# Output projection of a backbone layer: seven block products in another order, with other sums in PSUM

## The chip, the cores and the metric

The kernel runs on one core of a Trainium2 chip. The metric is device time in microseconds of one execution, and lower is better. The engines are named as in the profile: PE does the matmuls (PEld its weight loads), DVE the elementwise work on vectors, ACT the casts, copies, squares and roots, POOL (GpSimd) elementwise work in memory, and SP issues most transfers. PE writes its results to PSUM, which has eight banks; a bank holds 128 x 512 float32 values.

## The reference, cut to what matters

One layer: modulation, an input projection, a gated convolution and a neighbourhood attention side by side, a gated merge of the two branches, one output projection, a root-mean-square norm and a residual addition. Only the last steps are touched:

```python
merged = jax.nn.sigmoid(g_a) * y_a + jax.nn.sigmoid(g_b) * y_b
y = merged @ w_o                                  # (512, 1024) @ (1024, 1024)
x = x + gt[:, None, :] * _rmsnorm(y, post_g[i])
```

All of it is float32. The kernel writes a float32 operand as a high and a low part of a reduced type (F32R), and a product of two such operands as three matmuls: high by high, high by low, low by high.

## The kernel before

`layer` works in stages: modulation and norm, the input projection, attention, and then the stretch that matters here: the **merge** (the loop over `j` at L715, eight steps) and the **output projection** behind it (from L759).

*Merge.* Step `j` computes 128 of the 1024 merged features, transposed (features on partitions, the 512 tokens along the free axis). Two units of 24 matmuls each (L115 to L117, in `step_T`) multiply a chunk of 256 weight columns by the split operands `us` and `as`; L719 multiplies each result by its gate, and L726 adds the two to `m2[j]`. For `j` below 6 the gates of step `j + 2` are computed too (`merge_gates`, two more units, with the operands `h`). A chunk of weights is loaded by SP into `raw` (L84), cast on ACT (L70) and subtracted on DVE (L71), which gives its high and low part in a buffer `w`; there are two such buffers. `split` at L67 is the helper for all of these pairs, so L70 and L71 stand for every cast and every rest in the profile, told apart by the tile.

*Output projection.* The merged matrix is taken as 2 x 2 blocks (A11 and A12: the first 256 tokens by the first and last 512 features; A21 and A22: the last 256 tokens), and so is the weight `wo` (B11, B12, B21, B22, each 512 x 512, held as two tiles of 128 x 1024). Instead of eight block products there are seven (a scheme of the Strassen kind), on sums of blocks:

- row sums, made on DVE from the `m2` tiles: X1 = A22 - A21, S2 = -(X1) - A11, S3 = A11 - A21, S4 = -S2 - A12, up to sign;
- weight sums T1 to T4, made on DVE in place from the B tiles (`add_to`, L767);
- `moving` (L759) splits a weight block into a `w` buffer (two casts and two rests of 128 x 1024); `operand` and `split` do it for a row sum.

`both` issues one block product as two products of 12 matmuls (L773), one for each 128 tokens. The seven pairs follow one another: A11 B11 (bank pair `fa`), S3 T3 (`fd`), A12 B21 (`fb`), X1 T1 (added to `fd`), S2 T2 (added to `fa`), A22 T4 (added to `fa`), S4 B22 (added to `fd`). In between, ACT copies a running PSUM sum aside (`snap`, L801: P1s, P7s, U2s), and DVE adds such a copy to another bank to get a block of the output `ys` (L850, L864, L870, L875, L882). POOL subtracts P7s from U2s (L867). The last product is done in two halves of 256 columns (L881), both in the bank `fd[1]`, with L882 reading a half behind each.

*Norm and store.* `squares` (L803) has ACT square a block and sum it along the row (L804), and multiplies the block by `gpost` on POOL or DVE (L806). `partial` (L808) and `close` (L815) turn the sums into the reciprocal root of each row (a square root on ACT, L817, a reciprocal on DVE, L818), and L820 scales the row, adds the residual `xr` and leads to the store (L824).

What sets the order: each engine runs its instructions in one fixed order, in which the compiler's planner put them: it goes through the program in the order written and may take a later instruction first where an earlier one is not ready by its own estimate. So an instruction in the profile can stand far from its place in the text. A tile with a tag that another tile used before waits until the earlier one is no longer read. Reads and writes of the same PSUM bank are kept apart too, whichever columns they touch.

Of the kernel before, what the change touches and what calls it, by code (L numbers as in the profile page):

```python
# [27 lines left out]
def layer(ctx: ExitStack, tc, xp, ctxt, ctxT, cc, wmod, small, wfirst, win, wout, wo, rel, tab, out):  # L28
# [684 lines left out]
    h0, h1 = slice(0, 256), slice(256, S)

    for j in range(KT):  # L715
        w = chunk()
        g = G[j]
        for i in range(2):
            nc.vector.scalar_tensor_tensor(  # L719
                out=g[i], in0=g[i], scalar=1.0, in1=unit(w, i, ua[i]), op0=ALU.add, op1=ALU.mult  # L720
            )
# [4 lines left out]
        nc.vector.tensor_add(m2[j], g[0], g[1])  # L726
        if j < 4:
            split(A11[j // 2][:, 0, j % 2], A11[j // 2][:, 1, j % 2], m2[j][:, h0])
        if j == 1 or j == 3:
            q = j // 2  # L730
            x = cv.tile([P, S], F32, name="tb").rearrange("p (k c) -> p k c", k=2)
            nc.vector.tensor_sub(x, raws[q][:, :, h0], raws[q][:, :, h1])
            split(S3[q][:, 0], S3[q][:, 1], x)
        if j < 6:
            for _ in merge_gates(j + 2):
                pass
        if j == 4:

            nc.vector.tensor_scalar(out=gains[:, 0:4], in0=gains[:, 0:4], scalar1=0.5, scalar2=None, op0=ALU.mult)
            nc.vector.tensor_scalar(out=gains[:, 4:8], in0=gains[:, 4:8], scalar1=-0.5, scalar2=None, op0=ALU.mult)  # L740
            gpost = bp.tile([P, D], F32, name="gpost")
            for i in range(2):
                gb = cv.tile([P, S], F32, name="ta")
                ps = pj()
                for k in range(4):
                    n = 4 * i + k
                    nc.vector.tensor_copy(gb[:, k * P:(k + 1) * P], gains[:, n:n + 1].broadcast_to([P, P]))
                    nc.tensor.transpose(ps[:, k * P:(k + 1) * P], gb[:, k * P:(k + 1) * P], ident)
                nc.scalar.copy(gpost[:, i * S:(i + 1) * S], ps)
        if j == 5:  # L750

            B = {}
            for n, (r, c) in enumerate(((0, 0), (0, 1), (1, 1), (1, 0))):
                B[r, c] = [hp.tile([P, 2, S], F32, name=f"B{r}{c}{q}", tag=f"h{2 * n + q}") for q in range(2)]
                for q in range(2):
                    k = 4 * r + 2 * q
                    nc.sync.dma_start(B[r, c][q], wo[c, :, k:k + 2])

    def moving(src):  # L759
        t = wp.tile([P, 2, 4, S], F32R, name="w", bufs=2)  # L760
        for q in range(2):
            split(t[:, 0, 2 * q:2 * q + 2], t[:, 1, 2 * q:2 * q + 2], src[q])
        return t

    def add_to(dst, src):
        for q in range(2):
            nc.vector.tensor_add(dst[q], dst[q], src[q])  # L767

    def product(ps, a, w, start, t, cols=slice(0, S)):
        ts = slice(t * P, (t + 1) * P)  # L770
        for k in range(4):
            for x, y, o in ((0, 0, 0), (0, 1, 1), (1, 0, 2)):
                nc.tensor.matmul(  # L773
                    ps[:, cols], lhsT=a(x, k, ts), rhs=w[:, y, k, cols], start=start and k + o == 0,
                    stop=k == 3 and o == 2, skip_group_check=True,
                )

# [11 lines left out]
    fa, fd, fb = ([pj() for _ in range(2)] for _ in range(3))

    wB11 = moving(B[0, 0])
    add_to(B[0, 0], B[0, 1])
    add_to(B[0, 1], B[1, 1])
    wT3 = moving(B[0, 1])
    split(A2[3][:, 0], A2[3][:, 1], m2[7])
    for t in (2, 3, 0, 1):
        for i in range(2):
            nc.sync.dma_start(xr[t][i], xp[t * P:(t + 1) * P, i * S:(i + 1) * S])
# [4 lines left out]
    def squares(t, cols, n, k=1):  # L803
        nc.scalar.activation(sq[:, :cols.stop - cols.start], ys[t][:, cols], AF.Square, accum_out=sums[:, t, n:n + 1])  # L804
# [1 line left out]
        e.tensor_mul(ys[t][:, cols], ys[t][:, cols], gpost[:, cols])  # L806

    def partial(t, n, scalar):  # L808
        d = sums[:, t, 3:4]
        if scalar is None:  # L810
            nc.vector.tensor_scalar(out=d, in0=sums[:, t, n:n + 1], scalar1=0.25 / D, scalar2=EPS, op0=ALU.mult, op1=ALU.add)
# [18 lines left out]
    both(fa, stationary(A11), wB11, True, snap(lambda t: P1s[:, t], fa))  # L830
    wB21 = moving(B[1, 0])
    x2 = [cv.tile([P, S], F32, name="tb").rearrange("p (k c) -> p k c", k=2) for _ in range(2)]
    X1 = operand("X1", bp, ("us4", "us5"))
    S2 = operand("S2", bp, ("us6", "us7"))
    S4 = operand("S4", bp, ("as0", "as1"))
    for q in range(2):
        nc.vector.tensor_sub(x2[q], raws[2 + q][:, :, h1], raws[q][:, :, h1])
        split(X1[q][:, 0], X1[q][:, 1], x2[q])
    both(fd, stationary(S3), wT3, True, snap(lambda t: P7s[:, t], fd))
    wT1 = moving(B[0, 0])  # L840
    for q in range(2):
        nc.vector.scalar_tensor_tensor(
            out=x2[q], in0=x2[q], scalar=-1.0, in1=raws[q][:, :, h0], op0=ALU.mult, op1=ALU.subtract
        )
        split(S2[q][:, 0], S2[q][:, 1], x2[q])
    both(fb, a12, wB21, True)
    add_to(B[0, 0], B[1, 1])
    wT2 = moving(B[0, 0])
    for t in range(2):
        nc.vector.tensor_add(ys[t][:, c0], P1s[:, t], fb[t])  # L850
        squares(t, c0, 0)
        partial(t, 0, None)
    both(fd, stationary(X1), wT1, False)
    add_to(B[0, 0], B[1, 0])
    wT4 = moving(B[0, 0])
    for q in range(2):
        nc.vector.scalar_tensor_tensor(
            out=x2[q], in0=x2[q], scalar=-1.0, in1=raws[2 + q][:, :, h0], op0=ALU.mult, op1=ALU.subtract
        )
        split(S4[q][:, 0], S4[q][:, 1], x2[q])  # L860
    both(fa, stationary(S2), wT2, False, snap(lambda t: U2s[t], fa))
    wB22 = moving(B[1, 1])
    for t in range(2):
        nc.vector.tensor_add(ys[2 + t][:, c1], U2s[t], fd[t])  # L864
# [2 lines left out]
        nc.gpsimd.tensor_sub(U2s[t], U2s[t], P7s[:, t])  # L867
# [5 lines left out]
    s4 = stationary(S4)
    product(fd[0], s4, wB22, False, 0)
    nc.vector.tensor_add(ys[0][:, c1], U2s[0], fd[0])  # L875
    squares(0, c1, 1, 0)
    close(0, 1, ((0, 512), (512, 1024)))
    for i in range(2):
        cols = slice(256 * i, 256 * (i + 1))
        full = slice(S + 256 * i, S + 256 * (i + 1))  # L880
        product(fd[1], s4, wB22, False, 1, cols)  # L881
        nc.vector.tensor_add(ys[1][:, full], U2s[1][:, cols], fd[1][:, cols])  # L882
        squares(1, full, 1 + i, 0)
# [86 lines left out]
```

## Time and profile before

| | us |
|---|---|
| median of 3 runs | 732.17 (731.79 to 732.32) |
| the profiled execution | 731.5 |
| its span, first to last instruction | 729.7 |
| last pair of products of the merge ends, first pair of the projection starts | 677.7 |
| last matmul ends | 723.4 |

The times in the profile's lines are counted from the start of the span. A line of a timeline has the start, the duration of the group (for x2 or more from the first start to the last end), the engine, the line of the kernel, the operation, what it writes and reads, and in brackets how long the engine was idle before it and what released it. Neighbouring operations of one engine overlap a little, so that the distance of their starts is shorter than the duration shown.

### The profile page before, as it was taken

The numbers are of one execution on the slowest core, as the hardware profiler recorded it, in microseconds if no ns is written. First come the engines' busy times: TensorE is split into PE (matmuls) and PEld (weight loads), VectorE is DVE, ScalarE is ACT, GpSimd is POOL, SyncE is SP. The second block draws the span as 40 slices with busy tenths as digits, with TensorE's granted clock in tenths as the row PEclk, the third lists the DMA queues.
The fourth block names the chain that finished last, engine by engine and source line by source line (L and its number), as shares of the span: only waits on it lengthen the run. The fifth ranks groups of instructions, "written<-read, shape, count | busy, mean of one in ns | idle before, by whom it ended". The sixth has DMA issues, their size and how long they took to land.

```text
span 729.7 us, 9349 instructions
## 1 busy us (share of the span) xinstructions
PE 713.5 (98%) x3476; PEld 599.1 (82%) x3476; DVE 544.7 (75%) x1089; ACT 343.5 (47%) x631; POOL 11.6 (2%) x12
## 2 busy tenths in 40 slices
PE   8999999999999999999999999999999999999993
PEld 5888888888888888888888888888888888888882
DVE  7979989996997968779879689674934323326996
ACT  7574523563474654545536446443822222313553
POOL 0000000000000000000000000000000000000041
PEclk9999999999999999999999999999999999999997
DMA  9985982322221222131312212321133233265003
GB/s 351 406 301 180 310 295 91 106 64 92 73 65 67 72 75 71 58 101 44 130 58 74 72 58 73 101 88 58 58 115 114 76 100 116 88 202 201 29 1 116
DMA packets 26544, 86.63 MB, mean 119 GB/s; under 512 B 3073, under 2 KB 3329, under 8 KB 26498
## 3 DMA queue, kind: packets, MB, share of 16 engines
q1 hardware_dynamic: 26354, 85.90, 34.5%
q8 instruction: 27, 0.44, 0.3%
q14 instruction: 19, 0.16, 0.1%
q10 hardware_dynamic: 144, 0.13, 0.1%
HBM read 83.93 MB, written 2.10 MB: 118 GB/s over the span
## 4 chain that ended last, share of the span: by engine, by line
PE 91%; DVE 5%; ACT 1%; issue 1%; DMA 1%; SPq 0%; DVEq 0%; ACTq 0%
PE ps L117 20%; PE ps L115 20%; PE ps L116 20%; PE ps L128 6%; PE ps L600 4%; PE ps L584 4%; PE ps L133 3%; PE ps L552 3%; PE ps L773 2%; PE ps L141 2%; PE ps L307 2%; PE ps L311 2%; PE ps L308 2%; DVE w L71 2%; PE ps L561 1%; PE ps L146 1%
## 5 line engine op out<-in xcount | busy, mean ns | idle before, releaser
L115 PE MATMUL ps<-h,w 128*128 128x512 f32 x528 | 207.5, 393 | 0.0
L117 PE MATMUL ps<-h,w 128*128 128x512 f32 x528 | 206.0, 390 | 0.0
L116 PE MATMUL ps<-h,w 128*128 128x512 f32 x528 | 205.7, 390 | 0.0
L71 DVE TENSOR_TENSOR w<-raw,w 128x1024 fp32r<-128x1024 f32 x90 | 108.2, 1216 | 55.8 <-ACT w L70 55.6
L70 ACT CAST w<-raw 128x1024 fp32r<-128x1024 f32 x90 | 92.3, 1051 | 85.8 <-PE ps L117 64.4
L117 PEld LDWEIGHTS ps<-h,w 128*128 128x128 f32 x528 | 99.1, 188 | 20.9
L116 PEld LDWEIGHTS ps<-h,w 128*128 128x128 f32 x528 | 99.2, 188 | 20.3
L115 PEld LDWEIGHTS ps<-h,w 128*128 128x128 f32 x528 | 99.2, 188 | 20.0
L575 ACT ACTIVATE pt<-ps,m 128x512 f32<-128x512 f32 x64 | 44.3, 694 | 59.6 <-DVE m L572 59.6
L568 DVE CUSTOM_DVE_ANT_1 ps<-ps,bt 128x512 f32<-128x512 f32 x56 | 38.6, 700 | 15.1 <-PE ps L552 12.0
L71 DVE TENSOR_TENSOR TL<-ps,TH 128x512 fp32r<-128x512 f32 x64 | 42.7, 680 | 5.2 <-ACT TH L70 5.2
L719 DVE SCALAR_TENSOR_TENSOR g<-g,ps 128x512 f32<-128x512 f32 x16 | 11.0, 686 | 40.9 <-PE ps L117 40.9
L70 ACT CAST TH<-ps 128x512 fp32r<-128x512 f32 x64 | 35.1, 588 | 6.6 <-PE ps L584 6.4
L633 ACT ACTIVATE g<-ps 128x512 f32<-128x512 f32 x16 | 9.6, 598 | 57.8 <-PE ps L117 57.8
L584 PE MATMUL ps<-ident,pt 128*128 128x128 f32 x256 | 33.3, 272 | 0.0
L128 PE MATMUL ps<-w,h 128*128 128x512 f32 x128 | 32.7, 394 | 0.0
L577 DVE TENSOR_SCALAR pt<-pt,z 128x512 f32<-128x512 f32 x64 | 30.8, 482 | 1.0
L584 PEld LDWEIGHTS ps<-ident,pt 128*128 128x128 f32 x256 | 29.4, 140 | 2.3
L600 PE MATMUL ps<-TH,V 128*128 128x256 f32 (+1 forms) x96 | 28.5, 319 | 0.0
L600 PE MATMUL ps<-TL,V 128*128 128x256 f32 (+1 forms) x96 | 27.7, 318 | 0.0
L517 ACT ACTIVATE qd<-ta 64x512 fp32r<-64x512 f32 x32 | 20.2, 630 | 13.8 <-PE ps L561 7.1
L128 PEld LDWEIGHTS ps<-w,h 128*128 128x128 f32 x128 | 23.1, 189 | 4.3
(181 smaller groups left out, 1194.1 us busy)
## 6 DMA issues: line engine op xcount, KB each, us to landing
raw<-in_win SPq DMA_DIRECT2D x74, 512.0 KB, 4.2
wm<-in_wmod SPq DMA_DIRECT2D x34, 512.0 KB, 6.7
raw<-in_wout SPq DMA_DIRECT2D x16, 512.0 KB, 4.7
bt<-in_rel SPq DMA_DIRECT2D x16, 256.0 KB, 2.6
B<-in_wo SPq DMA_DIRECT2D x8, 512.0 KB, 7.1
fraw<-in_wfirst SPq DMA_DIRECT2D x8, 384.0 KB, 8.7
x<-in_xp SPq DMA_DIRECT2D x4, 512.0 KB, 4.9
xr<-in_xp SPq DMA_DIRECT2D x8, 256.0 KB, 3.0
```

The source lines that it names most:

```text
L70: nc.scalar.copy(H, src)
L71: nc.vector.tensor_sub(L, src, H.bitcast(F32))
L115: nc.tensor.matmul(ps, lhsT=H[:, k, cs], rhs=mH[k], start=k == 0, stop=False)
L116: nc.tensor.matmul(ps, lhsT=H[:, k, cs], rhs=mL[k], start=False, stop=False)
L117: nc.tensor.matmul(ps, lhsT=L[:, k, cs], rhs=mH[k], start=False, stop=k == KT - 1)
L128: nc.tensor.matmul(ps, lhsT=mH[k][:, ts], rhs=both[:, k].rearrange("p a c -> p (a c)"), start=k == 0, stop=False, skip_group_check=True,)
L133: nc.tensor.matmul(ps[:, :256], lhsT=mL[k][:, ts], rhs=H[:, k], start=False, stop=k == KT - 1, skip_group_check=True)
L568: nc.vector.tensor_tensor_reduce(out=s3, in0=s3, in1=bt[:, e::4 - e][:, 0:2], scale=1.0, scalar=-3.0e38, op0=ALU.add, op1=ALU.max, accum_o ...
L575: nc.scalar.activation(pt, s, AF.Exp, bias=m, scale=1.0, accum_out=z)
L577: nc.vector.tensor_scalar(out=pt, in0=pt, scalar1=z, scalar2=None, op0=ALU.mult)
L584: nc.tensor.transpose(tp[:, c], pt[:, c * P:(c + 1) * P], ident)
L600: nc.tensor.matmul(o3[:, dst], lhsT=V[p][:, kt, h], rhs=src(t), start=n == 0 and t is TH, stop=n == len(work) - 1 and t is TL,)
```

## The change

- The seven products come in the order A11 B11 (`fa`), A12 B21 (`fb`), S2 T2 (added to `fa`), X1 T1 (`fe`), S3 T3 (added to `fa`), S4 B22 (added to `fe`), A22 T4 (added to `fa`). The copies taken are P1s, U2s and U3s, all from `fa`. P7s and the two subtractions on POOL are gone.
- Three blocks of the output are an addition of a copy and a bank, as before. The fourth (tokens 256 to 511, first 512 columns) lies complete in `fa` at the end; the square and the product with `gpost` read it from PSUM, without an addition. The exception is the first half of its second 128 tokens, which is computed in a bank of its own (`ff`) and added to U3s.
- The weight sums T1 to T4 are made inside the merge loop at `j == 6`, and have tiles for T2 and T3; B11 and B12 are loaded at `j == 3` into new buffers, B22 and B21 at `j == 5`. T1 overwrites B11 after its split, T4 overwrites B12.
- The row sums X1 and S2 are made in place in the `m2` tiles (`sums1`): for the first half of the features at `j == 5`, for the second after the first product.
- All products with `gpost` are on DVE.
- The size of a DMA scratch area is set to 1024. The residual is loaded in another order.

The diff, cut to its core:

```diff
+    def total(dst, x, y):
+        for q in range(2):
+            nc.vector.tensor_add(dst[q], x[q], y[q])
+    B11, B12 = block("B11", bp, ("B0", "B1")), block("B12", bp, ("B2", "B3"))
+    def sums1(q):
+        nc.vector.tensor_sub(raws[q][:, :, h1], raws[2 + q][:, :, h1], raws[q][:, :, h1])
+        nc.vector.scalar_tensor_tensor(
+            out=raws[q][:, :, h0], in0=raws[q][:, :, h1], scalar=-1.0, in1=raws[q][:, :, h0],
+            op0=ALU.mult, op1=ALU.subtract,
+        )
...
+        if j == 3:
+            load_block(B11, 0, 0)
+            load_block(B12, 0, 1)
...
         if j == 5:
+            sums1(0)
+            B22, B21, T2, T3 = (block(n, hp, (f"h{2 * i}", f"h{2 * i + 1}")) for i, n in enumerate(("B22", "B21", "T2", "T3")))
+            load_block(B22, 1, 1)
+            load_block(B21, 1, 0)
+        if j == 6:
+            wB11 = moving(B11)
+            total(B11, B11, B12)
+            T1 = B11
+            total(T2, T1, B22)
+            total(T3, B12, B22)
+            T4 = B12
+            total(T4, T2, B21)
...
-        e = nc.gpsimd if k else nc.vector
-        e.tensor_mul(ys[t][:, cols], ys[t][:, cols], gpost[:, cols])
+        nc.vector.tensor_mul(y, src, gpost[:, cols])
...
+    both(fa, stationary(A11), wB11, True, snap(P1s, fa))
+    sums1(1)
+    for q in range(2):
+        split(S2[q][:, 0], S2[q][:, 1], raws[q][:, :, h0])
+    wT2 = moving(T2)
+    both(fb, a12, wB21, True)
+    for q in range(2):
+        split(X1[q][:, 0], X1[q][:, 1], raws[q][:, :, h1])
+    wT1 = moving(T1)
+    both(fa, stationary(S2), wT2, False, snap(U2s, fa))
+    wT3 = moving(T3)
...
+    both(fe, stationary(X1), wT1, True)
...
+    def block22(t):
+        snap(U3s, fa)(t)
+        nc.vector.tensor_add(ys[2 + t][:, c1], U3s[:, t], fe[t])
+    both(fa, stationary(S3), wT3, False, block22)
+    wT4 = moving(T4)
...
+    def block12(t):
+        nc.vector.tensor_add(ys[t][:, c1], U2s[:, t], fe[t])
+    both(fe, stationary(S4), wB22, False, block12)
+    for t in range(2):
+        squares(t, c1, 1)
+        close(t, 1, ((0, 512), (512, 1024)))
+    product(fa[0], a22, wT4, False, 0)
+    squares(2, c0, 1, fa[0])
+    close(2, 1, ((0, 512), (512, 1024)))
     for i in range(2):
         cols = slice(256 * i, 256 * (i + 1))
         if i == 0:
+            ff = pj()[:, :256]
+            product(None, a22, wT4, True, 1, cols, ff)
+            nc.vector.tensor_add(ys[3][:, cols], U3s[:, 1, cols], ff)
+            squares(3, cols, 1)
+            partial(3, 1, False)
+        else:
+            product(fa[1], a22, wT4, False, 1, cols)
+            squares(3, cols, 2, fa[1][:, cols])
+    close(3, 2, ((0, 512), (512, 768), (768, 1024)))
...
-    nc = bacc.Bacc("TRN2", target_bir_lowering=False, num_devices=1)
+    nc = bacc.Bacc("TRN2", target_bir_lowering=False, num_devices=1, dynamic_dma_scratch_size=1024)
```

More of the change, by code (lines that the diff above doesn't have):

```diff
@@ L703, in layer @@
     raws = [hp.tile([P, 2, S], F32, name=f"m{i}", tag=f"u{i}") for i in range(4)]
-    m2 = [raws[i % 4 // 2 + 2 * (i // 4)][:, i % 2] for i in range(KT)]
+    m2 = [raws[i // 2][:, i % 2] for i in range(KT)]
     def operand(name, pool, tags):
@@ L710, in stationary, with block, load_block, moving @@
         return lambda m, k, ts: t[k // 2][:, m, k % 2, ts]
+    def block(name, pool, tags):
+        return [pool.tile([P, 2, S], F32, name=f"{name}{q}", tag=t) for q, t in enumerate(tags)]
+    def load_block(t, r, c):
+        for q in range(2):
+            k = 4 * r + 2 * q
+            nc.sync.dma_start(t[q], wo[c, :, k:k + 2])
+    def total(dst, x, y):
+        for q in range(2):
+            nc.vector.tensor_add(dst[q], x[q], y[q])
+    def moving(src):
+        t = wp.tile([P, 2, 4, S], F32R, name="w", bufs=2)
+        for q in range(2):
+            split(t[:, 0, 2 * q:2 * q + 2], t[:, 1, 2 * q:2 * q + 2], src[q])
+        return t
     A11, S3 = operand("A11", hp, ("a0", "a1")), operand("S3", hp, ("a2", "a3"))
+    B11, B12 = block("B11", bp, ("B0", "B1")), block("B12", bp, ("B2", "B3"))
     h0, h1 = slice(0, 256), slice(256, S)
+    def sums1(q):
[4 more added lines that the diff above has]
+        )
     for j in range(KT):
@@ L750, in layer, with product @@
         if j == 5:
[L752 to L769, printed above, removed]
+            sums1(0)
[10 more added lines that the diff above has]
+            total(T4, T2, B21)
+    def product(ps, a, w, start, t, cols=slice(0, S), out=None):
         ts = slice(t * P, (t + 1) * P)
+        out = ps[:, cols] if out is None else out
         for k in range(4):
@@ L773, in product @@
                 nc.tensor.matmul(
-                    ps[:, cols], lhsT=a(x, k, ts), rhs=w[:, y, k, cols], start=start and k + o == 0,
+                    out, lhsT=a(x, k, ts), rhs=w[:, y, k, cols], start=start and k + o == 0,
                     stop=k == 3 and o == 2, skip_group_check=True,
@@ L784, in layer, with squares, partial @@
     ys = [bp.tile([P, D], F32, name=f"ys{t}", tag=f"as{2 + t}") for t in range(4)]
-    P1s, P7s = (bp.tile([P, 2, S], F32, name=n, tag=t) for n, t in (("P1s", "as6"), ("P7s", "as7")))
-    U2s = [cv.tile([P, S], F32, name="ta") for _ in range(2)]
+    P1s, U2s = (bp.tile([P, 2, S], F32, name=n, tag=t) for n, t in (("P1s", "as6"), ("U2s", "as7")))
     sq = cv.tile([P, S], F32, name="cs", bufs=1)
     sums = const.tile([P, 4, 4], F32, name="sums")
[L789 to L798, printed above, removed]
-    def snap(dst, ps):
-        return lambda t: nc.scalar.copy(dst(t), ps[t])
-    def squares(t, cols, n, k=1):
-        nc.scalar.activation(sq[:, :cols.stop - cols.start], ys[t][:, cols], AF.Square, accum_out=sums[:, t, n:n + 1])
-        e = nc.gpsimd if k else nc.vector
-        e.tensor_mul(ys[t][:, cols], ys[t][:, cols], gpost[:, cols])
-    def partial(t, n, scalar):
+    fa, fe, fb = ([pj() for _ in range(2)] for _ in range(3))
+    def snap(dst, ps):
+        return lambda t: nc.scalar.copy(dst[:, t], ps[t])
+    def squares(t, cols, n, src=None):
+        y = ys[t][:, cols]
+        src = y if src is None else src
+        nc.scalar.activation(sq[:, :cols.stop - cols.start], src, AF.Square, accum_out=sums[:, t, n:n + 1])
+        nc.vector.tensor_mul(y, src, gpost[:, cols])
+    def partial(t, n, first):
         d = sums[:, t, 3:4]
-        if scalar is None:
+        if first:
             nc.vector.tensor_scalar(out=d, in0=sums[:, t, n:n + 1], scalar1=0.25 / D, scalar2=EPS, op0=ALU.mult, op1=ALU.add)
@@ L828, in layer @@
     a22 = lambda m, k, ts: A2[k][:, m, ts.start + 256:ts.stop + 256]
[L830 to L835, printed above, removed]
+    split(A2[3][:, 0], A2[3][:, 1], m2[7])
+    wB21 = moving(B21)
+    for t in range(4):
+        for i in range(2):
+            nc.sync.dma_start(xr[t][i], xp[t * P:(t + 1) * P, i * S:(i + 1) * S])
+    both(fa, stationary(A11), wB11, True, snap(P1s, fa))
+    X1, S2, S4 = operand("X1", bp, ("us4", "us5")), operand("S2", bp, ("us6", "us7")), operand("S4", bp, ("as0", "as1"))
+    sums1(1)
     for q in range(2):
[L837 to L840, printed above, removed]
+        split(S2[q][:, 0], S2[q][:, 1], raws[q][:, :, h0])
+    wT2 = moving(T2)
+    both(fb, a12, wB21, True)
     for q in range(2):
[L842 to L848, printed above, removed]
+        split(X1[q][:, 0], X1[q][:, 1], raws[q][:, :, h1])
+    wT1 = moving(T1)
+    both(fa, stationary(S2), wT2, False, snap(U2s, fa))
+    wT3 = moving(T3)
     for t in range(2):
@@ L851, in layer @@
         squares(t, c0, 0)
[L852 to L855, printed above, removed]
+        partial(t, 0, True)
+    both(fe, stationary(X1), wT1, True)
     for q in range(2):
         nc.vector.scalar_tensor_tensor(
-            out=x2[q], in0=x2[q], scalar=-1.0, in1=raws[2 + q][:, :, h0], op0=ALU.mult, op1=ALU.subtract
-        )
-        split(S4[q][:, 0], S4[q][:, 1], x2[q])
-    both(fa, stationary(S2), wT2, False, snap(lambda t: U2s[t], fa))
@@ L862, in layer @@
-    wB22 = moving(B[1, 1])
+            out=raws[q][:, :, h0], in0=raws[q][:, :, h0], scalar=-1.0, in1=raws[2 + q][:, :, h0],
+            op0=ALU.mult, op1=ALU.subtract,
+        )
+        split(S4[q][:, 0], S4[q][:, 1], raws[q][:, :, h0])
+    wB22 = moving(B22)
+    U3s = bp.tile([P, 2, S], F32, name="U3s", tag="as6")
+    def block22(t):
[3 more added lines that the diff above has]
+    wT4 = moving(T4)
@@ L863, in layer @@
     for t in range(2):
-        nc.vector.tensor_add(ys[2 + t][:, c1], U2s[t], fd[t])
         squares(2 + t, c1, 0)
-        partial(2 + t, 0, None)
-        nc.gpsimd.tensor_sub(U2s[t], U2s[t], P7s[:, t])
-    both(fa, a22, wT4, False)
+        partial(2 + t, 0, True)
+    def block12(t):
+        nc.vector.tensor_add(ys[t][:, c1], U2s[:, t], fe[t])
+    both(fe, stationary(S4), wB22, False, block12)
     for t in range(2):
-        nc.vector.tensor_add(ys[2 + t][:, c0], P7s[:, t], fa[t])
-        squares(2 + t, c0, 1, 0)
-        close(2 + t, 1, ((0, 512), (512, 1024)))
@@ L873, in layer @@
[L873 to L877, printed above, removed]
+        squares(t, c1, 1)
[3 more added lines that the diff above has]
+    close(2, 1, ((0, 512), (512, 1024)))
     for i in range(2):
         cols = slice(256 * i, 256 * (i + 1))
[L880 to L883, printed above, removed]
@@ L884, in layer @@
         if i == 0:
-            partial(1, 1, True)
-    close(1, 2, ((0, 512), (512, 768), (768, 1024)))
+            ff = pj()[:, :256]
[7 more added lines that the diff above has]
+    close(3, 2, ((0, 512), (512, 768), (768, 1024)))
```

## The prediction

> **What bounds the kernel now.** I read the page's head first, then the windows of the output projection, then each engine's timeline there.
>
> ```profile
> span 729.7 us, 9349 instructions
> PE 713.5 (98%) x3476; PEld 599.1 (82%) x3476; DVE 544.7 (75%) x1089; ACT 343.5 (47%) x631; POOL 11.6 (2%) x12
> ```
>
> PE is busy for 98%, so only the 2% without it and what stands behind it can move. The windows say where they lie (columns: PE, PEld, DVE, ACT and POOL busy, granted PE clock, DMA share, GB/s):
>
> ```profile
> 640.00:667.00 27.00, 27.00 (x120) 22.36 (x120) 7.79 (x10) 5.09 (x7) 0.00 (x0) 1.00 0.65 237
> 667.00:710.30 43.30, 43.30 (x192) 35.86 (x191) 41.91 (x48) 24.89 (x38) 7.09 (x4) 1.00 0.07 25
> 710.30:715.00 4.70, 4.36 (x25) 3.58 (x23) 3.85 (x6) 2.30 (x4) 3.83 (x3) 1.00 0.00 0
> 715.00:720.40 5.40, 0.00 (x0) 0.00 (x0) 5.37 (x13) 2.03 (x6) 0.00 (x0) 0.89 0.41 156
> 720.40:723.40 3.00, 2.93 (x12) 2.63 (x12) 1.71 (x5) 0.51 (x2) 0.00 (x0) 0.50 0.64 247
> ```
>
> In the merge (640 to 667) DVE works 7.79 of 27.00 us; in the products (667 to 710.3) 41.91 of 43.30, as full as PE. From 715 to 720.4 PE does nothing and DVE is full: at the end DVE is the bound, and PE waits for it:
>
> ```profile
> 704.88 5.60 PE L773 MATMUL ps<-w,A 128*128 128x512 f32 x24
> 710.32 4.34 PE L773 MATMUL ps<-w,S 128*128 128x512 f32 x24
> 720.42 2.93 PE L773 MATMUL ps<-w,S 128*128 128x256 f32 x12 [5.77 <-DVE ys L882]
> ```
>
> A pair of products (24 matmuls) starts each 5.44 us (704.88 to 710.32) and its result is there after 5.60. The last 12 half-width matmuls wait 5.77 us, until L882 has read the first half of the same bank, and then run at clock 0.50. What follows them:
>
> ```profile
> 723.39 0.42 DVE L882 TENSOR_TENSOR ys<-ta,ps 128x256 f32<-128x256 f32 x1 [1.29 <-PE ps L773]
> 724.44 0.42 DVE L806 TENSOR_TENSOR ys<-ys,gpost 128x256 f32<-128x256 f32 x1 [0.64 <-ACT cs L804]
> 724.79 0.15 DVE L818 RECIPROCAL sums<-sums 128x1 f32<-128x1 f32 x1
> 724.98 1.55 DVE L820 SCALAR_TENSOR_TENSOR ys<-ys,sums,xr 128x512 f32<-128x512 f32 x3
> ```
> ```profile
> 723.90 0.42 ACT L804 ACTIVATE cs<-ys 128x256 f32<-128x256 f32 x1 [2.99 <-DVE ys L882]
> ```
>
> PE ends at 720.42 + 2.93 = 723.35, DVE at 724.98 + 1.55 = 726.53, the span at 729.7: 3.17 for the last store.
>
> **PE.** The seven products keep their matmuls: six pairs, one product of full width and two halves. Neither half waits for a reader of its bank now: the first has a bank of its own, and the second adds to a bank last read one pair of products earlier, by the copy U3s. Without the wait the seventh pair takes 5.60 like the others: 710.32 + 5.60 = 715.92, which is 7.43 us earlier. Behind it the addition is gone (the second half lies complete in PSUM): ACT began 0.55 after PE's end (723.90 against 723.35) and would begin some 0.1 after it. So 6.35 from PE's end to the span's end become 5.9, and PE alone would give a span of 721.8. That is the floor, and it holds only if DVE has nothing left over.
>
> **DVE, what one operation costs.** By the starts of neighbours:
>
> ```profile
> 678.74 0.68 DVE L842 SCALAR_TENSOR_TENSOR tb<-tb,m 128x512 f32<-128x512 f32 x1
> 679.35 0.68 DVE L726 TENSOR_TENSOR m<-g,g 128x512 f32<-128x512 f32 x1
> 679.95 2.35 DVE L71 TENSOR_TENSOR w<-B,w 128x1024 fp32r<-128x1024 f32 x2
> 682.22 0.68 DVE L71 TENSOR_TENSOR A<-m,A 128x512 fp32r<-128x512 f32 x1
> ...
> 717.97 1.41 DVE L820 SCALAR_TENSOR_TENSOR ys<-ys,sums,xr 128x512 f32<-128x512 f32 x2
> 719.30 0.68 DVE L806 TENSOR_TENSOR ys<-ys,gpost 128x512 f32<-128x512 f32 x1
> 719.90 0.15 DVE L818 RECIPROCAL sums<-sums 128x1 f32<-128x1 f32 x1
> ```
>
> 512 columns take 0.60 us (678.74 to 679.35; 719.30 to 719.90), 1024 take 1.135 (679.95 to 682.22 for two), a final L820 0.665 (717.97 to 719.30 for two), 256 columns 0.35 (724.44 to 724.79).
>
> **DVE, POOL idle.** While POOL works, DVE is slower:
>
> ```profile
> 699.00 1.66 DVE L767 TENSOR_TENSOR B<-B,B 128x1024 f32<-128x1024 f32 x1
> 700.58 0.14 DVE L811 TENSOR_SCALAR sums<-sums 128x1 f32<-128x1 f32 x1
> 700.64 2.25 DVE L767 TENSOR_TENSOR B<-B,B 128x1024 f32<-128x1024 f32 x1
> ...
> 707.49 4.22 DVE L71 TENSOR_TENSOR w<-B,w 128x1024 fp32r<-128x1024 f32 x2
> ```
> ```profile
> 697.51 2.06 POOL L806 TENSOR_TENSOR ys<-ys,gpost 128x512 f32<-128x512 f32 x1 [696.21 <-ACT cs L804]
> 699.98 1.84 POOL L806 TENSOR_TENSOR ys<-ys,gpost 128x512 f32<-128x512 f32 x1 [0.40 <-ACT cs L804]
> 707.11 3.52 POOL L867 TENSOR_TENSOR ta<-ta,P7s 128x512 f32<-128x512 f32 x2 [5.30 <-DVE ys L864]
> 710.60 3.53 POOL L806 TENSOR_TENSOR ys<-ys,gpost 128x512 f32<-128x512 f32 x2
> ```
>
> Against 1.175 each (2.35 for two) the additions lost 0.48 and 1.07 and the pair at 707.49 lost 1.87: 3.4 us, 2.0 of it ahead of 710.3 (of the pair, the 2.81 that lie there against 2.35). In exchange DVE gets POOL's four products with gpost, 4 x 0.60 = 2.4; the two subtractions disappear.
>
> The Trainium skill (SBUF — State Buffer, Who interferes with whom) calls the port that DVE and GpSimd share an exclusive lock for DVE operations with two SBUF inputs: the second to issue blocks until the first ends. The trace fits in part: the pair at 707.49 began behind a running POOL operation and lost 1.87. By the rule alone the loss could reach all of POOL's 10.95 us (the four rows above), and the time would be that of the floor; the rows show 3.4, and the sum uses those.
>
> **DVE, what moves under the merge.**
>
> ```profile
> 657.68 2.36 DVE L71 TENSOR_TENSOR w<-raw,w 128x1024 fp32r<-128x1024 f32 x2 [8.16 <-ACT w L70]
> 661.56 0.69 DVE L719 SCALAR_TENSOR_TENSOR g<-g,ps 128x512 f32<-128x512 f32 x1 [1.51 <-PE ps L117]
> 667.00 0.69 DVE L719 SCALAR_TENSOR_TENSOR g<-g,ps 128x512 f32<-128x512 f32 x1 [4.75 <-PE ps L117]
> ```
> ```profile
> 651.35 5.09 SPq L757 DMA_DIRECT2D B<-in_wo  x8
> ```
> ```profile
> 667.00 1.05 ACT L70 CAST w<-B 128x1024 fp32r<-128x1024 f32 x1 [8.40 <-PE ps L117]
> ```
>
> The idle 8.16, 1.51 and 4.75 us hide sums1(0) (its inputs exist after j = 5) and T3 = B12 + B22, 2 x 1.135 = 2.27. T1, T2 and T4 cannot go there: T1 overwrites B11, which the cast at 667.00 still reads, and that cast waits for a w buffer. So DVE has, from 667.0: L719 and L726 1.3, wB11 2.27, T1, T2, T4 6.81, that is until 677.4; then L719, A2[0..2], L719, L726 (six at 0.60) until 681.0, wB21 and A2[3], 2.87, until 683.9. The second pair of products starts at 683.1 and needs the second half of wB21 1.36 later, at 684.5 (six matmuls at 0.227): about 0.6 us to spare. Cover: PE's own first pair.
>
> Up to 710.3 DVE then has 41.91 (before) - 2.0 (POOL) - 2.27 (T3) - 0.6 (the one row sum that leaves this stretch) + 2.4 (gpost) + 0.7 (one more addition and two partial) = 40.1 us of 43.3: it fits with 3.2 to spare for waits.
>
> The loads: B11 and B12, 2 MB, may go out as soon as their buffers exist, in front of a chunk's load on SP. At 237 GB/s (the first window) that holds a chunk back 8.8 us at most; a chunk's values are ready at 660.04 (657.68 + 2.36), 6.5 ahead of PE's need at 666.6, and its cast stood waiting for PE before that. Cost nothing; without that cover 2.3. The order of xr, the changed DMA scratch size (the page has no queue fed by POOL) and the sums in place: nothing, as nothing waits for them.
>
> **DVE, the end.** The sixth pair's result is there at 704.88 + 5.60 = 710.5. From then DVE owes: the addition for ys[1] 0.60, two gpost products 1.20, two reciprocals 0.30, four L820 2.66; for the full product of the seventh pair 0.60 + 0.15 + 1.33; for the halves 0.35 + 0.35 + 0.10 and 0.35 + 0.19 + 1.55. Sum 9.73: 720.2. Waits inside: the table load,
>
> ```profile
> 713.27 1.28 ACT L817 ACT_TABLE_LOAD   x1
> 714.57 0.29 ACT L817 ACTIVATE sums<-sums 128x1 f32<-128x1 f32 x1
> ```
>
> which holds the first reciprocal 1.6 us, of which DVE can fill about two thirds (0.5 left; bounds 0 and 1.6), and the last square ahead of the last reciprocal (0.4). I take 0.9: DVE ends at 721.1, 5.4 before 726.53. Span 724.3. The profiled execution took 731.5, so 726.1; the median of the runs shown is 732.17, 0.67 above that execution: **726.8 us**. So of 7.9 that PE frees, DVE keeps 2.5.
>
> **Rivals.**
> *A, PE is the bound* (chance 0.15): ACT and DVE finish the early rows in time, span 721.8, time 732.17 - 7.9 = 724.3. For it: the 3.2 us to spare. Against: 9.73 us of work behind a result that comes 5.4 before PE's end.
> *B, the sums run late* (0.16): T3 stays behind the cast at 667.00 as the other sums do (its B22 lands late, or it is ordered so). Then 2.27 more stand ahead of wB21, 0.6 is spare, PE waits 1.7 and the whole end moves: 728.5. For it: the sums are written ahead of j = 7 in the program.
> *C, a new wait of PE, the slower side* (0.16): the sixth pair adds into fe, which DVE must read first (block22: product, copy on ACT, addition). The second product of the fifth pair ends at 705.0 and its bank is needed at 704.88 + 2.72 = 707.6. If DVE has the addition behind both halves of wT4, whose buffer comes free at 705.0 too, it ends at 705.0 + 1.05 (cast) + 2.27 + 0.6 = 708.9, and PE waits 1.3. That alone gives 728.1. But 5.77 us of idle PE ended in clock 0.50; should the wait cost the clock too, 36 matmuls at 0.227 take 8.2 more: 726.8 + 9.5 = 736.3. It decides from 6.9 us of loss (slower), and from 3.9 the time is within 0.2%: 0.07 for that, 0.09 for slower.
> The Trainium skill (TensorE: Matmul & The Clock Gate, Part 1) has the clock fall only after an idle window of some 3.4 us. The trace agrees that 5.77 was enough; whether 1.3 is, no row shows. By the rule C would stop at 728.1.
> *D, the half still waits* (0.06), for a reason that the code does not show: PE resumes when DVE has read the first half, about 717.6, 2.93 at the low clock, 5.9 behind: span 726.4, time 728.9.
>
> **Numbers.** Forecast 0.47, A 0.15, B 0.16, C 0.16, D 0.06. Faster by over 0.2% (about what a measurement of this kernel can tell from no change): 0.47 + 0.15 + 0.16 + 0.06 = 0.84; within 0.07; slower 0.09. The range goes from below A (723.6) to above B and D (730.2), leaving out C.
>
> **What would show it.** Right: no idle of PE in the seven products, PE's end near 716, clock 1.00 to the end, DVE without gaps from 710 to its end near 721, POOL empty there, no 1024-column operation of DVE over 1.3 us. Wrong: PE waiting at the second or sixth pair (B, C), DVE idle while the last product runs (A), a wait ahead of the last 12 matmuls (D).

## The result, and the profile after

| | before | changed |
|---|---|---|
| median of 6 runs, us | 732.08 (731.79 to 732.32) | 726.99 (726.57 to 727.27) |
| ratio to before, 95% interval | | 0.993 (0.9917 to 0.9943) |
| the profiled execution, its span, us | 731.5, 729.7 | 726.93, 725.2 |

The changed kernel is 5.1 us faster; 726.8 had been forecast, in a range of 723.6 to 730.2. The page's head after the change:

```profile
span 725.2 us, 9329 instructions
PE 711.3 (98%) x3476; PEld 597.1 (82%) x3476; DVE 542.6 (75%) x1091; ACT 344.1 (47%) x631; POOL 0.7 (0%) x6
```

PE has the same 3476 matmuls, and POOL does nothing in the stretch below. The windows of the output projection, cut at the same times as those of before (columns: PE, PEld, DVE, ACT and POOL busy, granted PE clock, DMA share, GB/s):

```profile
640.00:667.00 27.00, 27.00 (x121) 22.35 (x120) 10.96 (x12) 5.09 (x6) 0.00 (x0) 1.00 0.48 164
667.00:710.30 43.30, 43.30 (x193) 35.87 (x192) 40.16 (x52) 25.36 (x38) 0.00 (x0) 1.00 0.08 25
710.30:715.00 4.70, 4.70 (x28) 4.16 (x27) 3.50 (x7) 4.08 (x10) 0.00 (x0) 1.00 0.01 3
715.00:720.40 5.40, 1.48 (x13) 1.28 (x11) 5.28 (x14) 1.28 (x5) 0.00 (x0) 1.00 0.72 274
720.40:723.40 3.00, 0.00 (x0) 0.00 (x0) 1.23 (x3) 0.00 (x0) 0.00 (x0) 0.50 0.56 204
```

Under the merge DVE works 10.96 us instead of 7.79, in the products 40.16 instead of 41.91. PE is done in the fourth stretch, while DVE is still full there (5.28 of 5.40) and runs over into the fifth. PE's timeline has no wait left:

```profile
678.09 11.04 PE L799 MATMUL ps<-w,A 128*128 128x512 f32 x48
688.97 5.60 PE L799 MATMUL ps<-w,S 128*128 128x512 f32 x24
694.41 5.60 PE L799 MATMUL ps<-w,X 128*128 128x512 f32 x24
699.85 11.04 PE L799 MATMUL ps<-w,S 128*128 128x512 f32 x48
710.73 5.75 PE L799 MATMUL ps<-w,A 128*128 128x512 f32 x36
```

The seven pairs run through, two of them in each of the rows of 11.04. PE ends at 710.73 + 5.75 = 716.48, where before it ended at 723.35: 6.9 us earlier. The kernel gained 5.1. Where the rest is, DVE's timeline shows (L71 makes the rest of a split, L889 adds the blocks of ys[0] and ys[1], L823 multiplies by `gpost`, L835 is the reciprocal, L837 the final scaling):

```profile
701.14 2.36 DVE L71 TENSOR_TENSOR w<-B,w 128x1024 fp32r<-128x1024 f32 x2 [1.15 <-ACT w L70]
...
709.34 0.68 DVE L823 TENSOR_TENSOR ys<-ys,gpost 128x512 f32<-128x512 f32 x1
...
710.01 0.68 DVE L889 TENSOR_TENSOR ys<-U2s,ps 128x512 f32<-128x512 f32 x1
710.93 0.69 DVE L889 TENSOR_TENSOR ys<-U2s,ps 128x512 f32<-128x512 f32 x1 [0.25 <-PE ps L799]
711.54 0.69 DVE L823 TENSOR_TENSOR ys<-ys,gpost 128x512 f32<-128x512 f32 x1
713.14 0.16 DVE L835 RECIPROCAL sums<-sums 128x1 f32<-128x1 f32 x1 [0.92 <-ACT sums L834]
...
719.37 0.42 DVE L823 TENSOR_TENSOR ys<-ps,gpost 128x256 f32<-128x256 f32 x1
719.88 0.16 DVE L835 RECIPROCAL sums<-sums 128x1 f32<-128x1 f32 x1
720.08 1.54 DVE L837 SCALAR_TENSOR_TENSOR ys<-ys,sums,xr 128x512 f32<-128x512 f32 x3
```

The sixth pair's second bank is read at 710.93, and from there DVE works without a pause except for 0.92 us (and some 0.1 at 719.8), up to 720.08 + 1.54 = 721.62: 5.1 us behind PE's end. The 0.92 us are a wait for ACT's square root. ACT's timeline shows why:

```profile
710.78 0.64 ACT L822 ACTIVATE cs<-ys 128x512 f32<-128x512 f32 x1 [2.18 <-DVE ys L889]
...
711.52 1.28 ACT L834 ACT_TABLE_LOAD   x1
712.82 0.29 ACT L834 ACTIVATE sums<-sums 128x1 f32<-128x1 f32 x1
```

ACT stood idle for 2.18 us, squared the block that L889 had just made, and only then loaded the table for the root.

For comparisons of traces one thing has to be taken out. The first product pair starts at 677.68 in the profile of before, at 678.09 in that of the changed kernel, and anywhere from 677.75 to 678.78 in the runs below, though most of these alter nothing ahead of it. So DVE's end is counted from that start, called S: **48.85 us before, 43.53 after**. From 667.00 to its end DVE was busy for 55.29 us before (the last four of the windows, 52.84, and 2.45 behind them) and 50.17 after (the last four rows above). Its idle time there hardly changed (4.24 of 59.53 before, 4.45 of 54.62 after, or 4.04 if it is counted from 667.41, which lies as far ahead of S as 667.00 did before). So of the 5.32 us by which DVE's end came closer to S, 5.12 are work that left DVE's queue in this stretch.

### The profile page after: what moved, and what is told of

Its sections match the earlier page's. It is cut to its first block, busy times and chain, and to the rows that moved or that the text cites. A ratio compares the mean times of both kernels' runs of the same rounds, so it can differ in the third digit from the quotient of the medians.

```text
span 725.2 us, 9329 instructions
## 1 busy us (share of the span) xinstructions
PE 711.3 (98%) x3476; PEld 597.1 (82%) x3476; DVE 542.6 (75%) x1091; ACT 344.1 (47%) x631; POOL 0.7 (0%) x6
## 4 chain that ended last, share of the span: by engine, by line
PE 94%; DVE 2%; DMA 1%; ACT 1%; SPq 0%; issue 0%; DVEq 0%; ACTq 0%
PE ps L117 20%; PE ps L116 20%; PE ps L115 20%; PE ps L128 6%; PE ps L600 4%; PE ps L799 4%; PE ps L584 4%; PE ps L133 3%; PE ps L552 3%; PE ps L141 2%; PE ps L307 2%; PE ps L311 2%; PE ps L308 2%; DMA fraw<-in_wfirst 1%; PE ps L561 1%; PE ps L146 1%
## 5 line engine op out<-in xcount | busy, mean ns | idle before, releaser
L71 DVE TENSOR_TENSOR w<-raw,w 128x1024 fp32r<-128x1024 f32 x90 | 108.3, 1218 | 47.3 <-ACT w L70 47.1
L71 DVE TENSOR_TENSOR TL<-ps,TH 128x512 fp32r<-128x512 f32 x64 | 42.8, 682 | 5.2 <-ACT TH L70 5.2
```

The costliest lines, as they stand in the source:

```text
L71: nc.vector.tensor_sub(L, src, H.bitcast(F32))
```

## The experiments

Theory: DVE's queue sets the end, and PE's end has slack. Rivals: PE sets it; the gain is that of the bank alone; POOL's idling brings most of it. The table has every run; "DVE end - S" is from the profiled execution.

| run | built on | median us (range) | ratio (95%) | DVE end - S |
|---|---|---|---|---|
| the half on a shared bank | changed | 728.09 (727.46-728.79) | 0.9946 (0.9933-0.9958) | 44.27 |
| POOL takes its products again | changed | 726.10 (725.90-726.49) | 0.9919 (0.9906-0.9933) | 43.01 |
| less DVE at the end | changed | 726.19 (725.90-726.36) | 0.9919 (0.9906-0.9933) | 42.93 |
| less PE at the end | changed | 727.07 (726.62-727.36) | 0.9933 (0.9920-0.9947) | 43.53 |
| own bank alone | before | 730.66 (730.17-731.23) | 0.9981 (0.9973-0.9990) | 47.47 |
| POOL idle alone | before | 728.98 (728.81-729.63) | 0.9959 (0.9947-0.9972) | 46.15 |
| T3 late | changed | 727.71 (727.57-728.04) | 0.9942 (0.9929-0.9954) | 44.28 |
| another order | changed | 726.01 (725.28-726.09) | 0.9915 (0.9901-0.9928) | 42.28 |
| root early | changed | 726.15 (725.94-726.22) | 0.9921 (0.9908-0.9935) | 42.57 |
| root early, POOL products | changed | 726.01 (725.84-726.65) | 0.9922 (0.9908-0.9936) | 42.58 |
| another order, root early | changed | 725.33 (725.17-725.77) | 0.9912 (0.9899-0.9926) | 41.79 |

All ratios are to the kernel before. Steps of 0.1% between variants lie inside these intervals; where one is read below, the ranges and DVE's end carry it.

**Less PE, less DVE.** Two kernels, each lighter at the end on one engine:

```diff
# less PE, in the loop of product()
+        if a is a22 and o == 1:
+            continue
# less DVE, in squares()
-        nc.vector.tensor_mul(y, src, gpost[:, cols])
+        if not (t < 2 and n == 1):
+            nc.vector.tensor_mul(y, src, gpost[:, cols])
```

> The changed kernel leaves out the high by low matmuls of the seventh pair (12 of 36 instructions), so that PE ends about 1.8 us earlier. Theory (DVE is the bound): the last reciprocal waited only about 0.1 for PE's and ACT's side, so 726.9. Rival A (PE is the bound): 1.8 less, 725.2.

> The changed kernel leaves out the product with gpost of the last columns of rows 0 and 1: two DVE operations of 0.60 us, both behind the sixth pair. Theory (DVE is the bound at the end): the first of them stands ahead of a wait of 0.92 us for the root and saves nothing, the second saves its 0.60: 726.4. Rival A (PE is the bound): 727.0.

With less PE, the last product on PE's timeline, and the last scaling on DVE's:

```profile
710.40 3.88 PE L801 MATMUL ps<-w,A 128*128 128x512 f32 x24
```
```profile
719.75 1.54 DVE L839 SCALAR_TENSOR_TENSOR ys<-ys,sums,xr 128x512 f32<-128x512 f32 x3
```

The last pair takes 3.88 us instead of 5.75, and nothing comes of it: 727.07 against 726.99, and DVE ends 43.53 us behind S, as in the changed kernel. With less DVE, the first reciprocal and the last scaling:

```profile
713.18 0.16 DVE L836 RECIPROCAL sums<-sums 128x1 f32<-128x1 f32 x1 [1.52 <-ACT sums L835]
...
719.51 1.54 DVE L838 SCALAR_TENSOR_TENSOR ys<-ys,sums,xr 128x512 f32<-128x512 f32 x3
```

Of two products of 0.60 us, one stood in front of the wait for the root, and the wait grew by as much (0.92 to 1.52). The other counts: DVE ends 0.60 earlier, and the time falls by 0.8. So the end is DVE's, and the last 1.87 us of PE's work (5.75 - 3.88) are worth nothing to it.

**The bank, taken back and alone.** In the changed kernel both halves go to `fa[1]`; in the kernel before the first half gets a bank of its own:

```diff
# shared bank
-            ff = pj()[:, :256]
-            product(None, a22, wT4, True, 1, cols, ff)
-            nc.vector.tensor_add(ys[3][:, cols], U3s[:, 1, cols], ff)
-            squares(3, cols, 1)
+            product(fa[1], a22, wT4, False, 1, cols)
+            squares(3, cols, 1, fa[1][:, cols])
# own bank alone
+    nc.vector.tensor_add(U2s[1][:, :256], U2s[1][:, :256], fd[1][:, :256])
...
-        product(fd[1], s4, wB22, False, 1, cols)
-        nc.vector.tensor_add(ys[1][:, full], U2s[1][:, cols], fd[1][:, cols])
+        o = pj()[:, :256] if i == 0 else fd[1][:, cols]
+        product(o, s4, wB22, i == 0, 1, cols)
+        nc.vector.tensor_add(ys[1][:, full], U2s[1][:, cols], o)
```

> The changed kernel with both last halves in fa[1] again, and so without the addition of the first half (0.35 us of DVE less). Theory (the bank's own worth is limited, since DVE is the bound at the end): the second half waits until DVE has read the first, about 717.7; that is 2.7 us of idle PE. If the clock stays, PE ends near 719.4 and the time rises by some 0.5 to 727.5; if the clock falls to 0.50 as it did before the change, PE ends near 720.7 and the time is 728.8. Rival (the bank alone made the gain): 732. Rival (the bank is worth nothing): 726.7.

> The kernel before with only the last half's own bank (the first half goes to a free bank; the running sum under it is added to U2s earlier, 0.35 us more of DVE). Theory: PE ends near 716 instead of 723.4, but DVE still has 9.5 us of work from 715.0 on, plus 0.35 and a wait of 0.4, so it ends near 725.1 instead of 726.5: 730.7. Rival (the bank makes the whole gain): 727.

With the shared bank PE waits again. Its timeline, and the windows of the wait and of what follows (columns as above):

```profile
710.49 4.31 PE L799 MATMUL ps<-w,A 128*128 128x512 f32 x24
717.55 1.96 PE L799 MATMUL ps<-w,A 128*128 128x256 f32 x12 [2.75 <-DVE ys L823]
```
```profile
714.80:717.55 2.75, 0.00 (x2) 0.00 (x1) 2.75 (x8) 0.47 (x2) 0.00 (x0) 1.00 0.58 219
717.55:718.50 0.95, 0.95 (x8) 0.95 (x9) 0.95 (x2) 0.00 (x0) 0.00 (x0) 1.00 1.01 384
718.50:719.00 0.50, 0.50 (x6) 0.50 (x5) 0.38 (x2) 0.00 (x0) 0.00 (x0) 0.79 0.37 139
719.00:719.60 0.60, 0.50 (x3) 0.21 (x1) 0.00 (x0) 0.06 (x1) 0.00 (x0) 0.50 0.94 362
```

The wait is 2.75 us and not 5.77, since DVE reads the first half earlier than it did before, and it costs 1.1 us in the median (0.74 in DVE's end; the profiled execution is the fastest of the five). The granted clock is still 1.00 for the first microsecond behind the wait, and falls to 0.50 while the last matmuls run. The Trainium skill (TensorE: Matmul & The Clock Gate, Part 1) lets the clock fall after an idle window of about 3.4 us, whose place in time is not fixed. Here the clock fell after an idle time of only 2.75 us; the measurement decides.

With the bank alone, in the kernel before, PE waits for nothing, yet the time falls by only 1.3 us (730.66 against 731.96 in the same series). PE's last pair and DVE's last scaling:

```profile
711.42 5.78 PE L773 MATMUL ps<-w,S 128*128 128x512 f32 x36
```
```profile
708.59 4.24 DVE L71 TENSOR_TENSOR w<-B,w 128x1024 fp32r<-128x1024 f32 x2
...
724.71 1.54 DVE L820 SCALAR_TENSOR_TENSOR ys<-ys,sums,xr 128x512 f32<-128x512 f32 x3
```

PE ends at 717.20 and DVE at 726.25, nine microseconds behind. This is the prediction's main statement in a single run: a wait of 5.77 us with a throttled clock behind it disappears, and DVE's queue keeps most of it (one more addition of 256 columns, some 0.35, is part of the edit). A pair of rests took 4.24 us there, beside POOL's work, as the 4.22 did in the kernel before.

**POOL, alone and taken back.** In the kernel before, POOL's products with `gpost` and its subtraction go to DVE; in the changed kernel the products go back:

```diff
# POOL idle alone (kernel before)
-        e = nc.gpsimd if k else nc.vector
-        e.tensor_mul(ys[t][:, cols], ys[t][:, cols], gpost[:, cols])
+        nc.vector.tensor_mul(ys[t][:, cols], ys[t][:, cols], gpost[:, cols])
...
-        nc.gpsimd.tensor_sub(U2s[t], U2s[t], P7s[:, t])
+        nc.vector.tensor_sub(U2s[t], U2s[t], P7s[:, t])
# POOL takes its products again (changed kernel), in squares()
-        nc.vector.tensor_mul(y, src, gpost[:, cols])
+        (nc.gpsimd if n == 0 else nc.vector).tensor_mul(y, src, gpost[:, cols])
```

> The kernel before with only POOL's six operations on DVE. DVE gets 6 x 0.60 = 3.6 us and sheds 4.1 of slowed operations, so its sum stays. Theory: the planner puts the reading of the first half earlier, so that the wait of PE at the end shrinks and DVE's own two waits there (1.9) partly go: 730.0 to 731.5. Rival (contention is the main loss): 3.4 less, 728.7. Rival (nothing): 732.1.

> The changed kernel with the four early products with gpost (first columns of rows 0 and 1, last columns of rows 2 and 3) on POOL again. DVE loses 2.4 us of work and gains what POOL's port costs it. Theory: all four lie ahead of the crowded end, where DVE has some 4 us of gaps, so the time is 727.0 to 728.0. Rival (the contention with POOL was the main loss): 3.4 us more, 730.4.

Both were misses, and both kernels came out faster than expected: POOL's idling is worth more than was set in the kernel before, and less than nothing in the changed one. Alone, idling POOL brings 3.0 us (728.98 against 731.96), more than twice the bank. The number lies near the rival's 728.7, but what the theory named is there too. In PE's timeline the wait of the last half shrinks, and DVE reads the first half early:

```profile
715.22 1.70 PE L773 MATMUL ps<-w,S 128*128 128x256 f32 x12 [0.51 <-DVE ys L881]
```
```profile
714.74 0.42 DVE L881 TENSOR_TENSOR ys<-ta,ps 128x256 f32<-128x256 f32 x1
```

The same reading in the profile of the kernel before:

```profile
719.97 0.40 DVE L882 TENSOR_TENSOR ys<-ta,ps 128x256 f32<-128x256 f32 x1
```

It is 0.51 us and not 5.77, though the bank is still shared: PE resumes at 715.22 and not at 720.42, as DVE has read the first half that much sooner. Two things changed for DVE: none of its operations is slowed any more, and the planner has put L881 ahead of all scalings, where L882 stood behind four of them. How much of the 3.0 us is the one and how much the other, this run does not separate.

In the changed kernel, POOL's products make it faster instead of slower. POOL's timeline, and DVE's beside it:

```profile
694.15 3.22 POOL L823 TENSOR_TENSOR ys<-ys,gpost 128x512 f32<-128x512 f32 x2 [692.85 <-ACT cs L822]
...
708.71 1.91 POOL L823 TENSOR_TENSOR ys<-ys,gpost 128x512 f32<-128x512 f32 x1 [2.46 <-ACT cs L822]
```
```profile
694.49 1.72 DVE L870 SCALAR_TENSOR_TENSOR m<-m,m 128x512 f32<-128x512 f32 x1
...
696.47 3.11 DVE L71 TENSOR_TENSOR w<-T,w 128x1024 fp32r<-128x1024 f32 x2 [0.20 <-ACT w L70]
...
701.18 2.36 DVE L71 TENSOR_TENSOR w<-B,w 128x1024 fp32r<-128x1024 f32 x2 [0.39 <-ACT w L70]
...
709.45 0.68 DVE L889 TENSOR_TENSOR ys<-U2s,ps 128x512 f32<-128x512 f32 x1
...
712.58 0.16 DVE L835 RECIPROCAL sums<-sums 128x1 f32<-128x1 f32 x1 [0.32 <-ACT sums L834]
```

POOL still slows DVE: one sum takes 1.72 us instead of 0.68, a pair of rests 3.11 instead of 2.36. But that is at 694 to 700, ahead of a pause that DVE has anyway (1.15 us before 701.14 in the changed kernel, 0.39 here). What counts comes later: the product of row block 3 no longer stands ahead of the addition L889, which starts at 709.45 instead of 710.01, and the square, the table load and the first reciprocal all come 0.56 earlier (712.58 against 713.14). If that is the reason, a table load moved out of that place makes POOL's products worthless. Two runs ask that:

```diff
# root early: behind the loop that calls partial(2 + t, 0, True)
+    nc.scalar.activation(sums[:, 3, 1:2], sums[:, 3, 0:1], AF.Sqrt)
# the same with POOL products for the row blocks 2 and 3
+        (nc.gpsimd if t > 1 and n == 0 else nc.vector).tensor_mul(y, src, gpost[:, cols])
```

> The changed kernel with one more square root of a single column on ACT behind the square of the last columns of row block 3, so that the table load (1.28 us) falls into ACT's idle 2.18 us ahead of the crowded end. Its result is overwritten. Theory (the load stands in the chain block12 addition, square, load, root, reciprocal, and DVE waits 0.92 us for it at 713.1): the wait goes, DVE starts its contiguous work 0.9 earlier, 726.1. Rival (DVE's work alone sets the end and the wait is filled elsewhere): 727.0.

> As e9, and the products with gpost of the last columns of rows 2 and 3 on POOL. Theory (e2 was faster because without such a product ahead of it the block12 addition, and with it the table load, came 0.56 us earlier): with the load out of the chain POOL brings nothing more, 726.1 as e9. Rival (each 0.60 us taken off DVE counts): 0.6 to 0.9 less than e9, 725.3.

The additional root's result is written over later; it brings the table in early. ACT's timeline, and DVE's:

```profile
708.80 1.28 ACT L887 ACT_TABLE_LOAD   x1
```
```profile
712.33 0.15 DVE L835 RECIPROCAL sums<-sums 128x1 f32<-128x1 f32 x1
...
719.31 1.54 DVE L837 SCALAR_TENSOR_TENSOR ys<-ys,sums,xr 128x512 f32<-128x512 f32 x3
```

The load lies in ACT's idle time, the reciprocal waits for nothing, and the time is 726.15. Against the changed kernel that is 0.84 less in the medians (0.66 by the ratios, as the kernel before was 0.33 faster in this series) and 0.96 less in DVE's end, for 0.92 us of waiting. With POOL's products besides, it is 726.01 in an overlapping range, and DVE ends 42.58 us behind S against 42.57: nothing more. That fits the reason given.

**T3 late (rival B).** Copies of a few elements tie T3 to T2, so that T3 falls behind the cast at the merge's end:

```diff
+            for q in range(2):
+                nc.vector.tensor_copy(T3[q][:, :, 0:1], T2[q][:, :, 0:1])
             total(T3, B12, B22)
```

> The changed kernel with T3 forced behind T2 (one column of T2 is copied into T3 first and then overwritten), so that its 2.27 us no longer lie in the idle time of the merge but ahead of the split of wB21. Theory (what stands ahead of the sixth pair's end moves the end): the second and third pairs have 1.1 to 1.2 us to spare in the trace, PE waits about 1.3, and the time is 728.3. Rival (DVE's 4.4 us of gaps take it up): 727.0.

```profile
684.86 5.38 PE L801 MATMUL ps<-w,A 128*128 128x512 f32 x22 [0.36 <-DVE w L71]
690.07 5.60 PE L801 MATMUL ps<-w,S 128*128 128x512 f32 x24
```

PE's timeline shows a wait two matmuls into the second pair, and the third pair starts 11.63 us behind S (678.44 in this run) instead of 10.88: 0.75 us later, which is what the time gained too, 0.72 in the medians and 0.75 in DVE's end. Not all of it is waiting: the row shows 0.36 us of idle, and the 22 matmuls behind it take 5.38 us, where 5.15 would be usual (5.60 for 24, less 2 x 0.227). The rival was real, and its price was half of what was set.

**Another order, and the root early.** To take work out from behind the sixth pair, S4 B22 goes ahead of S3 T3. ACT copies X1 T1 aside (`X1s`), the blocks of rows 0 and 1 are closed one pair earlier, and the rests of T4 come later:

```diff
+    both(fe, stationary(X1), wT1, True, snap(X1s, fe))
...
+    both(fe, stationary(S4), wB22, False, block12)
+    wT4 = moving(T4)
+    def block22(t):
+        nc.vector.tensor_add(ys[2 + t][:, c1], X1s[:, t], fa[t])
...
+    both(fa, stationary(S3), wT3, False, block22)
```

> The changed kernel with S4 B22 as the fifth pair and S3 T3 as the sixth: X1 T1 is copied aside, rows 0 and 1 are complete a pair earlier, and about 3 us of DVE work (two reciprocals, four L837 of the changed kernel) move from behind the sixth pair to ahead of it. Theory (DVE's work behind the sixth pair sets the end): DVE ends at 719 to 720 instead of 721.6 and the time is 724.5 to 725.5; the floor that PE sets is near 724.4. Rival (DVE is as full ahead of the sixth pair, so that wT4 comes late and PE waits): 727 to 728.

```profile
705.80 1.28 ACT L834 ACT_TABLE_LOAD   x1
...
707.29 1.99 ACT L70 CAST w<-B 128x1024 fp32r<-128x1024 f32 x2
```

726.01: short of the expected gain. ACT's timeline shows a reason. The root now comes early enough to stand in front of the casts of T4, and they start 28.81 us behind S (707.29) where the changed kernel has them 27.89 behind (705.98); the rests behind them are late, and the last scaling with them. With one root more, behind the first row blocks' sums (`nc.scalar.activation(sums[:, 1, 1:2], sums[:, 1, 0:1], AF.Sqrt)`), the load goes out of the way:

> e8 with the extra root behind the square of the first columns of row block 1, so that the table load falls into ACT's idle 1.35 us between the two copies of X1s. Theory: the load no longer delays the casts of wT4 and the first reciprocal; of DVE's waits between 700 and 708 in e8 (1.74, 0.85, 0.32) the last two shrink, 0.3 to 0.8 less than e8: 725.2 to 725.7. Rival (e8 is bound by its work behind the sixth pair, which stays): 726.0.

```profile
698.70 1.28 ACT L874 ACT_TABLE_LOAD   x1
...
705.60 1.98 ACT L70 CAST w<-B 128x1024 fp32r<-128x1024 f32 x2
```
```profile
718.33 1.54 DVE L837 SCALAR_TENSOR_TENSOR ys<-ys,sums,xr 128x512 f32<-128x512 f32 x3
```

725.33 us, ratio 0.9912 (0.9899 to 0.9926): the fastest of all, below both kernels, with a range apart from that of the early root alone in the same series. Against the other order without the extra root the ranges overlap (another series), and DVE's end, 0.49 earlier, carries the comparison. DVE ends at 719.87, still 3.4 us behind PE (716.47 by the same 5.75 for the last pair, from 710.72).

## Why the prediction came out

| step | predicted | measured |
|---|---|---|
| first pair to PE's end | 38.24 (677.68 to 715.92) | 38.39 (678.09 to 716.48) |
| DVE's work from 667.0 to 710.3 | 40.1 | 40.54 (667.41 to 710.71, as far from S) |
| second pair's operand ready in time | yes, 0.6 to spare | yes; 1.1 by the same rule, some 1.6 by the run with T3 late |
| sixth pair's end to DVE's end | 9.73 and 0.9 of waits | 10.69 (710.93 to 721.62) |
| of that, the wait for the root | 0.5 | 0.92 |
| and the wait for the last square | 0.4 | 0.1 (719.37 + 0.42 to 719.88) |
| first pair to DVE's end | 43.42 (677.68 to 721.1) | 43.53 |
| the last store | 3.17 | 3.58 (725.2 - 721.62) |

**Right** was the argument: count DVE's queue behind the sixth pair, operation by operation, and let that set the end instead of PE's wait. Of the 6.9 us by which PE ended earlier, the kernel kept what DVE could follow. Rival A (PE is the bound) fell with the run that has less PE: a shorter product, the same time. Rival C did not occur, as PE's timeline has no wait at the sixth pair. Rival D neither; the run with the shared bank makes its case, and there PE resumed at 717.55, as set (717.6), with 728.09 instead of 728.9. Rival B did not occur by itself. Forced, it cost 0.75 and not 1.7: DVE was 2.4 us later there (2.27 for T3 and two small copies) and PE lost 0.75, so some 1.6 were to spare and not 0.6. In part this is because DVE was sooner than predicted (in the changed kernel wB21 is done at 683.79, and by the prediction's rule it was needed 6.80 behind S, at 684.89), and for the rest because wB21 is needed later than the prediction had it.

**Off by a little**, with errors that cancel: everything ahead of the projection lay 0.41 later in this profiled execution, and the last store took 0.41 more, so the span is 725.2 and not 724.3. On the other side, the prediction had added 0.67 for the distance of the profiled execution before to its median; for the changed kernel that distance is 0.06 (726.99 against 726.93). The two waits at the end cancel as well: together they were set at 0.9 and came to 1.0, but the one was nearly twice its size and the other a quarter. The closeness of 726.8 to 726.99 is partly this accident; DVE's end, 43.42 against 43.53, is the fair test.

**Mis-sized** was the term "DVE, POOL idle": 3.4 us of slowed operations against 2.4 of products handed back, a gain of 1.0. It left out one slowed operation of the kernel before, which took 1.39 us instead of 0.68 while POOL worked from 710.60 to 714.13, so the slowed ones come to 4.1:

```profile
713.28 1.39 DVE L806 TENSOR_TENSOR ys<-ys,gpost 128x512 f32<-128x512 f32 x1 [0.85 <-ACT cs L804]
```

Ahead of 710.3 the count of DVE's time held (40.54 against 40.1). As a price the term did not: POOL's idling was worth 3.0 by itself in the kernel before and minus 0.9 in the changed one. So the rival that it brings most of the gain fits the kernel before and not the changed one. The sum treated operations as equal wherever they stood. In the kernel before, all the slowed ones lay on the chain that ended last, which runs through DVE from 690.3 on; POOL's subtractions did not. In the changed kernel they would lie ahead of a pause, while the product of 0.60 that DVE took over stands ahead of the table load, a wait that the prediction itself had set at 0.5 and which became 0.92.

The parts do not add up to the change: alone, the bank brings 1.3 and POOL's idling 3.0, together 4.3 of 5.1. They can't simply be added either, for both shorten the same wait of PE, and no run has the two together. What the other order of products, T3 under the merge, the addition that falls away, the loads and the scratch size bring was not tried alone. **Open** are two things: what of POOL's 3.0 in the kernel before is contention and what is order; and why the last store is 3.5 to 3.6 us behind DVE's end in the changed kernel and in all that is built on it, against 3.15 to 3.3 in those built on the kernel before. That POOL's products gain 0.9 in the changed kernel and DVE's end shows 0.5 of it is no riddle: the profiled execution there is the slowest of its four (726.49), 0.44 below that of the changed kernel.

## What to carry to other kernels

When the profile shows PE waiting for DVE at the end, add up what DVE still owes behind the last results: that sum, and not the length of PE's wait, is what removing the wait leaves. Work handed from one engine to another has no price of its own; look whether the operation, or the one that it slows, stands ahead of a pause or on the chain to the end. In these runs the table load for the last function costs nothing if an earlier use of that function puts it where ACT idles and no cast is queued behind it.
